# A deeper ring of split weights for SwiGLU, and silu in one ScalarE instruction, in a float32 encoder block on one core

## The chip, the cores and the metric

The kernel runs on one core of one Trainium2 chip. The metric is the device time of one execution in microseconds (us); lower is better. The median of three runs of the kernel before is 1158.89 us (1158.38 to 1160.23). About 0.2% of that, 2.3 us, is the bound used below between a change and no change.

The engines are named as in the profile: PE is TensorE's matmuls, PEld its weight loads, DVE is VectorE, ACT is ScalarE, POOL is GpSimd, and SP (SPq for its queue) is SyncE, which here issues the DMAs that bring the weights.

## The reference, cut to what matters

One encoder layer over 256 rows of width 2048: two kinds of attention heads side by side, a cross attention into 256 memory rows, and a SwiGLU feed-forward of hidden width 5632. All data is float32.

```python
x = x + concat(out_mla, out_diff) @ w_out
x = x + cross_attention(rms_norm(x), rms_norm(mem)) @ w_xo
hf = rms_norm(x, g_ffn)
x = x + (silu(hf @ w_gate) * (hf @ w_up)) @ w_down     # w_gate, w_up: 2048 x 5632
return rms_norm(x, g_final)
```

silu(v) is v times sigmoid(v). The change lies in the feed-forward and in the tile pools that it uses.

## The kernel before, in words

**Three matmuls for one.** A float32 operand is split into a high part of type float32r and the rest, so that each product is three matmuls (`mm`, L91 to L93: high by high, high by low, low by high). The split is two instructions (`split_into`, L99 and L100): ACT rounds the operand into the high tile, then DVE subtracts the high tile from the operand into the low tile. Every weight of the kernel passes through this split.

**The two rings.** A weight piece of 1 MB lands by one DMA from SP in a raw tile, `wraw` (128 x 2048 float32, a ring of 3). It is then split by 1024 columns into a tile `wh` and a tile `wl` (rings of 4 each). A ring's tile is taken again only after its last reader is done: a split waits until PE has used the tile four splits back, and a DMA waits until both parts of the raw tile three back have been split. The rings are in pool `wp` for the whole kernel; pool `act` (24 tiles) holds activations, and pool `sb` a ring of 7 small tiles called `nat` (128 x 512), used by attention and SwiGLU alike.

**Order of the work.** The program is handed to a planner that simulates the engines and fixes the order of instructions on each engine before the run; program order is the priority. DMAs of weights are kept in program order. In the trace, matmuls of neighbouring tiles are interleaved by that plan.

**SwiGLU.** It starts with 512 hidden columns done plainly (`narrow_chunk`: two projections of `x2T`, the unnormalized rows), during which the normalized and split rows `x2n` and `forms` are made (`normalized_pairs`). Then come five chunks of 1024 hidden columns (`wide_chunk`): a gate projection, silu of it, an up projection, the product `h`, and its transposes on PE. The chunks are in three groups (one narrow and one wide chunk, two wide, two wide), and each group ends with its part of the down projection. The last group's down projection ends the kernel, with the final norm.

**Plain and summed pairs.** A wide projection (`wide_project`) runs over pairs of 128-row blocks of the contraction. A plain pair takes 8 products (24 matmuls). A summed pair uses sums of weight blocks and of activation blocks, and takes 7 products (21 matmuls); it accumulates four of them apart, in PSUM tiles `q`, which five DVE instructions per projection join (L737 to L740 with an ACT copy L736, or their like in `wide_add`). Of the 8 pairs of a gate or up projection 2 are summed; the whole SwiGLU has 28 summed pairs. For a summed pair DVE makes sums of the raw weight blocks in a tile `tsum` (L707, L711, L712), and four splits follow: three into the ring, the last into an extra pair of tiles of its own (`wh2`, `wl2` in pool `wsum`, one each). `wsum` is opened where attention's pool `soft` has been closed.

**PSUM.** Eight banks: four `acc` tiles for accumulation and four `ps` tiles for `q`, for transposes and the like. The four `acc` tiles of the first wide projection are the ones that the narrow chunk's gate (`ga`) and up (`ua`) results leave.

**Silu.** In `narrow_chunk` ACT computes the sigmoid of the scaled accumulator into a `nat` tile `sg` (L808) and DVE multiplies accumulator, scale and `sg` (L809); a second DVE instruction multiplies by the up result into `h` (L811). In `wide_chunk`, four times per chunk, ACT computes the sigmoid into `sg` (L824) and DVE multiplies it onto the gate result (L825).

Of the kernel before, what the change touches and what calls it, by code (L numbers as in the profile page):

```python
# [19 lines left out]
P = 128  # L20
# [54 lines left out]
def encoder_block(ctx: ExitStack, tc: tile.TileContext, a, out):  # L75
    nc = tc.nc
    PS = bass.MemoryType.PSUM
    const = ctx.enter_context(tc.tile_pool(name="const", bufs=1))
    wp = ctx.enter_context(tc.tile_pool(name="wp", bufs=3))
# [4 lines left out]
    pps = ctx.enter_context(tc.tile_pool(name="pps", bufs=4, space=PS))  # L84
    tables = ExitStack()
    tp = tables.enter_context(tc.tile_pool(name="tp", bufs=1))


    def mm(o, l, r, start, stop):

        nc.tensor.matmul(o, l.h, r.h, start=start, stop=False)  # L91
        nc.tensor.matmul(o, l.h, r.l, start=False, stop=False)  # L92
        nc.tensor.matmul(o, l.l, r.h, start=False, stop=stop)  # L93
# [13 lines left out]
    def act_tile(shape=(P, 4, S), name="act"):  # L107
# [2 lines left out]
            act.tile(list(shape), F32R, name=name + "_l", tag="act"),  # L110
        )

    def weights(src, fine=False, pool=None, before_k=None, cut=None, raw=None):

        nk, ncols = src.shape[1:]
        begun = raw is not None
        if not begun:  # L120
            raw = wp.tile([P, 2048], F32, name="wraw", tag="wraw", bufs=3)
        raw = raw[:, :nk * ncols].rearrange("p (k c) -> p k c", k=nk)
        step = 1 if fine else nk
        for k in range(0, nk, step):
            if before_k is not None:
                before_k(k)
            if begun and k == 0:
                continue
            tc.keep_in_program_order(nc.sync.dma_start(out=raw[:, k:k + step, :], in_=src[:, k:k + step, :]))
        ks = []  # L130
        step = max(1, 1024 // ncols // 2 * 2)
        for k in range(0, nk, step):
            n = min(step, nk - k)
            if pool:
                w = pool((P, n, ncols), "w")
            else:
                w = [wp.tile([P, 1024], F32R, name=x, tag=x, bufs=4)[:, :n * ncols].rearrange("p (k c) -> p k c", k=n)
                     for x in ("wh", "wl")]
                w = Split(*w)
# [24 lines left out]
        return accs  # L164

    def nat(name):
        return sb.tile([P, 512], F32, name=name, tag="nat", bufs=7)

    def ps_tile(name):
        return pps.tile([P, 512], F32, name=name, tag="ps")  # L170
# [13 lines left out]


    LAT = KVL + DR
    lat_raw = wp.tile([P, 2048], F32, name="wraw", tag="wraw", bufs=3)
# [14 lines left out]
    posi = const.tile([P, NT], I32, name="posi")  # L202
    invf = const.tile([P, NF], F32, name="invf")
# [59 lines left out]

    posf = const.tile([P, NT], F32, name="posf")
    nc.gpsimd.tensor_copy(out=posf, in_=posi)
    ang = tp.tile([P, NT, NF], F32, name="ang")
    for tt in range(NT):
# [78 lines left out]
    cosr = const.tile([P, NT, 2, DR // 2], F32, name="cosr")  # L348
    sinr = const.tile([P, NT, 2, DR // 2], F32, name="sinr")
    cosd = const.tile([P, NT, 2, DD // 2], F32, name="cosd")  # L350
    sind = const.tile([P, NT, 2, DD // 2], F32, name="sind")

    def latents_normalized():
        cqs = [nat("cq") for _ in range(NT)]
# [152 lines left out]
    gdb = const.tile([P, DV], F32, name="gdb")  # L507
# [129 lines left out]
    def pair_raw(src):  # L637
        raw = wp.tile([P, 2048], F32, name="wraw", tag="wraw", bufs=3)
        raw = raw.rearrange("p (b c) -> p b c", b=4)
        tc.keep_in_program_order(nc.sync.dma_start(out=raw, in_=src))  # L640
        return raw

    def w_tile(n=2, pool=None):

        pool, tags, bufs = (wp, ("wh", "wl"), 4) if pool is None else (pool, ("wh2", "wl2"), 1)
        return Split(*[pool.tile([P, 1024], F32R, name=x, tag=x, bufs=bufs)[:, :n * 512].rearrange(
            "p (b c) -> p b c", b=n) for x in tags])

    def split_blocks(src, pool=None):
        w = w_tile(src.shape[1], pool)  # L650
        split_into(w, src)
        return w

    class Pair:

# [24 lines left out]
    def wide_project(pairs, src, order, leave, join):  # L680

        accs = [[pacc.tile([P, 512], F32, name="acc", tag="acc") for _ in range(2)] for _ in range(NT)]
        used = [[False] * 2 for _ in range(NT)]
        summed = [i for i in order if pairs[i].forms is not None]  # L690
        Q = {}
        for n, i in enumerate(order):
            stop = n == len(order) - 1
            raw = pair_raw(src[i])
            if i not in summed:
                w = [split_blocks(raw[:, 2 * k:2 * k + 2, :]) for k in range(2)]
                for tt in range(NT):
                    for oc in range(2):
                        for k in range(2):
                            mm(accs[tt][oc], pairs[i].at(k, tt), w[k][:, oc, :], not used[tt][oc], stop and k == 1)  # L700
# [6 lines left out]
            nc.vector.tensor_tensor(out=t[:, 0:2, :], in0=raw[:, 1:3, :],  # L707
                                    in1=raw[:, 0:1, :].to_broadcast([P, 2, 512]), op=ALU.add)
            t13 = split_blocks(t[:, 0:2, :])
            b21 = split_blocks(raw[:, 3:4, :])  # L710
            nc.vector.tensor_tensor(out=t[:, 2, :], in0=t[:, 0, :], in1=raw[:, 2, :], op=ALU.add)  # L711
            nc.vector.tensor_tensor(out=t[:, 3, :], in0=t[:, 2, :], in1=raw[:, 3, :], op=ALU.add)  # L712
# [3 lines left out]
            mm(Q[1], A11, b11[:, 0, :], *own)  # L716
            mm(accs[0][1], S3, b11[:, 1, :], False, stop)
            mm(Q[5], S5, t13[:, 0, :], *own)
            mm(Q[7], S7, t13[:, 1, :], *own)
            mm(accs[0][0], A12, b21[:, 0, :], False, stop)  # L720
            mm(Q[6], S6, t24[:, 0, :], *own)
            mm(accs[1][0], A22, t24[:, 1, :], False, stop)
# [76 lines left out]
    def narrow_chunk(c):  # L799

        ga = project(x2T, [a["w_gate0"][0, i] for i in range(4)])
        xn = normalized_pairs()
        ua = project(x2T, [a["w_up0"][0, i] for i in range(4)])
        t = act_tile(name="hT")
        for tt in range(NT):
            r = rstdf[:, tt:tt + 1]
            sg = nat("sg")
            nc.scalar.activation(sg, ga[tt], AF.Sigmoid, scale=r)  # L808
            nc.vector.scalar_tensor_tensor(out=sg, in0=ga[tt], scalar=r, in1=sg, op0=ALU.mult, op1=ALU.mult)  # L809
            h = nat("h")  # L810
            nc.vector.scalar_tensor_tensor(out=h, in0=ua[tt], scalar=r, in1=sg, op0=ALU.mult, op1=ALU.mult)  # L811
            transposed(t, h, tt, 4)
        return [Pair(t[:, 0:2, :]), Pair(t[:, 2:4, :])], xn
# [3 lines left out]
    def wide_chunk(c, spare):  # L817

        g = wide_result(xn, a["w_gu"][c, 0], GU_SEQ)
        for tt in range(NT):  # L820
            for oc in range(2):
                sg = nat("sg")
                gs = g[tt][:, oc, :]
                nc.scalar.activation(sg, gs, AF.Sigmoid)  # L824
                nc.vector.tensor_tensor(out=gs, in0=gs, in1=sg, op=ALU.mult)  # L825
        u = wide_result(xn, a["w_gu"][c, 1], GU_SEQ)
        t = act_tile(name="hT")
        pts = []
# [177 lines left out]
```

## Time and profile before

| quantity | value |
|---|---|
| median of the three runs | 1158.89 us |
| the profiled execution's own time | 1158.9 us |
| its span, first to last instruction | 1157.1 us |
| granted TensorE clock, mean | 0.999 |
| matmuls | 5510 |
| bytes moved by DMA | 222.13 MB, mean 192 GB/s |

The profile is a page about one execution, and a trace that can be asked for details. Durations of PE instructions overlap, since matmuls are pipelined and their ends are modelled; so the distance from one matmul's start to the next one's says more than its duration. In a row of a group of instructions, the columns are the source line, the engine, the operation, output and inputs by name, the shape, the count, then busy time in us, the mean of one in ns, and the idle time ahead of them with what ended it. In a row of a table by stage, each engine's busy time in us is followed by the number of its instructions in that stretch.

### The profile page before, as it was taken

The numbers are of one execution on the slowest core, as the hardware profiler recorded it, in microseconds if no ns is written. First come the engines' busy times: TensorE is split into PE (matmuls) and PEld (weight loads), VectorE is DVE, ScalarE is ACT, GpSimd is POOL, SyncE is SP. The second block draws the span as 40 slices with busy tenths as digits, with TensorE's granted clock in tenths as the row PEclk, the third lists the DMA queues.
The fourth block names the chain that finished last, engine by engine and source line by source line (L and its number), as shares of the span: only waits on it lengthen the run. The fifth ranks groups of instructions, "written<-read, shape, count | busy, mean of one in ns | idle before, by whom it ended". The sixth has DMA issues, their size and how long they took to land.

```text
span 1157.1 us, 14401 instructions
## 1 busy us (share of the span) xinstructions
PE 1148.1 (99%) x5510; PEld 961.7 (83%) x5510; DVE 901.3 (78%) x1197; ACT 611.0 (53%) x863; POOL 69.3 (6%) x81
## 2 busy tenths in 40 slices
PE   9999999999999999999999999999999999999997
PEld 7888888888888888888888888888888888888887
DVE  7698766586867776978888787797888788798873
ACT  6755454554665565655444554564544554554552
POOL 4920000001000000000000000000000000000021
PEclk9999999999999999999999999999999999999999
DMA  9565344435755445465565555645556555555651
GB/s 356 215 218 189 113 145 168 161 146 206 272 212 182 146 149 187 174 218 182 185 214 184 206 184 192 218 181 183 202 179 223 204 181 202 192 220 202 210 204 73
DMA packets 33764, 222.13 MB, mean 192 GB/s; under 512 B 4128, under 2 KB 4896, under 8 KB 8992
## 3 DMA queue, kind: packets, MB, share of 16 engines
q1 hardware_dynamic: 32256, 216.86, 52.4%
q0 software_dynamic: 864, 3.15, 0.7%
q10 hardware_dynamic: 576, 1.21, 0.3%
q8 instruction: 43, 0.70, 0.2%
q14 instruction: 25, 0.20, 0.1%
HBM read 219.11 MB, written 2.10 MB: 191 GB/s over the span
## 4 chain that ended last, share of the span: by engine, by line
PE 98%; DMA 1%; issue 0%; DVE 0%; SPq 0%; ACT 0%; POOLq 0%; POOL 0%; DVEq 0%; ACTq 0%
PE acc L92 28%; PE acc L91 28%; PE acc L93 28%; PE q L91 2%; PE q L92 2%; PE q L93 2%; PE pt L315 2%; PE ppt L462 1%; DMA wraw<-in_w_in_lat 1%; PE psc L93 1%; PE psc L91 1%; PE psc L92 1%; PE pt L838 0%; PE acckv L93 0%; PE acckv L92 0%
## 5 line engine op out<-in xcount | busy, mean ns | idle before, releaser
L99 ACT CAST wh<-wraw 128x1024 fp32r<-128x1024 f32 (+2 forms) x399 | 399.2, 1013 | 383.1 <-PE acc L93 346.7
L100 DVE TENSOR_TENSOR wl<-wraw,wh 128x1024 fp32r<-128x1024 f32 (+2 forms) x399 | 469.0, 1184 | 166.3 <-ACT wh L99 164.4
L92 PE MATMUL acc<-wl,x2n_h 128*128 128x512 f32 x480 | 185.5, 390 | 0.0
L93 PE MATMUL acc<-wh,x2n_l 128*128 128x512 f32 x480 | 185.2, 389 | 0.0
L91 PE MATMUL acc<-wh,x2n_h 128*128 128x512 f32 x480 | 160.3, 390 | 0.0
L93 PEld LDWEIGHTS acc<-wh,x2n_l 128*128 128x128 f32 x480 | 90.1, 188 | 18.8
L91 PEld LDWEIGHTS acc<-wh,x2n_h 128*128 128x128 f32 x480 | 90.1, 188 | 18.8
L92 PEld LDWEIGHTS acc<-wl,x2n_h 128*128 128x128 f32 x480 | 90.1, 188 | 18.7
L92 PE MATMUL acc<-wl,hT_h 128*128 128x512 f32 (+1 forms) x272 | 103.7, 381 | 0.0
L93 PE MATMUL acc<-wh,hT_l 128*128 128x512 f32 (+1 forms) x272 | 103.5, 381 | 0.0
L91 PE MATMUL acc<-wh,hT_h 128*128 128x512 f32 (+1 forms) x272 | 89.4, 382 | 0.0
L92 PE MATMUL acc<-wl,x0T_h 128*128 128x512 f32 x224 | 88.2, 395 | 0.0
L93 PE MATMUL acc<-wh,x0T_l 128*128 128x512 f32 x224 | 87.8, 393 | 0.0
L91 PE MATMUL acc<-wh,x0T_h 128*128 128x512 f32 x224 | 87.4, 396 | 0.3 <-ACT x0T_h L102 0.3
L99 ACT CAST wh<-tsum 128x1024 fp32r<-128x1024 f32 x56 | 58.3, 1047 | 42.2 <-DVE tsum L712 30.8
L100 DVE TENSOR_TENSOR wl<-tsum,wh 128x1024 fp32r<-128x1024 f32 x56 | 67.9, 1218 | 9.2 <-ACT wh L99 9.1
L91 PEld LDWEIGHTS acc<-wh,hT_h 128*128 128x128 f32 x272 | 51.2, 188 | 9.9 <-issue 0.2
L93 PEld LDWEIGHTS acc<-wh,hT_l 128*128 128x128 f32 x272 | 51.2, 188 | 9.6
L92 PEld LDWEIGHTS acc<-wl,hT_h 128*128 128x128 f32 x272 | 51.2, 188 | 9.4
L91 PEld LDWEIGHTS acc<-wh,x0T_h 128*128 128x128 f32 x224 | 42.2, 189 | 9.2 <-ACT x0T_h L102 1.2
L92 PEld LDWEIGHTS acc<-wl,x0T_h 128*128 128x128 f32 x224 | 42.3, 189 | 7.9 <-DVE wl L100 0.4
L93 PEld LDWEIGHTS acc<-wh,x0T_l 128*128 128x128 f32 x224 | 42.2, 188 | 7.6
(363 smaller groups left out, 2005.9 us busy)
## 6 DMA issues: line engine op xcount, KB each, us to landing
wraw<-in_w_gu SPq DMA_DIRECT2D x80, 1024.0 KB, 4.8
wraw<-in_w_dn SPq DMA_DIRECT2D x36, 1024.0 KB, 4.8
wraw<-in_w_in SPq DMA_DIRECT2D x24, 1024.0 KB, 4.8
wraw<-in_w_out SPq DMA_DIRECT2D x16, 1024.0 KB, 4.8
wraw<-in_w_down SPq DMA_DIRECT2D x8, 1024.0 KB, 4.8
wraw<-in_w_in_lat SPq DMA_DIRECT2D x7, 832.0 KB, 7.8
wraw<-in_w_xk SPq DMA_DIRECT2D x4, 1024.0 KB, 6.1
wraw<-in_w_xq SPq DMA_DIRECT2D x4, 1024.0 KB, 4.8
```

The costliest lines, as they stand in the source:

```text
L91: nc.tensor.matmul(o, l.h, r.h, start=start, stop=False)
L92: nc.tensor.matmul(o, l.h, r.l, start=False, stop=False)
L93: nc.tensor.matmul(o, l.l, r.h, start=False, stop=stop)
L99: last_cast[0] = nc.scalar.copy(out=dst.h, in_=src).ins
L100: last_split[0] = nc.vector.tensor_tensor(out=dst.l, in0=src, in1=dst.h.bitcast(F32), op=ALU.subtract).ins
L315: nc.tensor.transpose(out=pt[:, j * P:(j + 1) * P], in_=src[:, j * P:(j + 1) * P], identity=ident)
L462: nc.tensor.transpose(out=pt[:, kt * S + tt * P:kt * S + (tt + 1) * P], in_=p[:, tt, kt * P:(kt + 1) * P], identity=ident)
```

## The change

It does the following:

- `wraw`, `wh` and `wl` become `Ring` objects: lists of named slots of one tile each, taken in turn. A ring can be given more slots from another pool; the new ones are taken first.
- Tiles that only attention needs (`nat`, the rotary tables, `posi`, `invf`, `posf`, `gdb`) move to a pool `early`, which is closed with `soft` at the end of attention. In that space a pool `late` is opened: three more tiles `wh` and `wl` each, a ring of 3 `nat` tiles in place of 7, and `tsum` (three blocks in place of four).
- From SwiGLU on the rings of `wh` and `wl` have 7 tiles; the extra pair `wh2`, `wl2` goes. The ring of `wraw` keeps 3.
- The sums of a summed pair are made in another order, partly in place in the raw tile: two additions come before the pair's first split, two after it. The splits are of 1024, 1024, 1024 and 512 columns, all into the ring. The seven products keep their operands and come in another order.
- Silu is one ACT instruction with the function Silu. In `wide_chunk` it works in place on the gate result; the DVE product with the sigmoid goes.

```diff
-            raw = wp.tile([P, 2048], F32, name="wraw", tag="wraw", bufs=3)
+            raw = w_raw.next()
...
+    class Ring:
...
+        def more(self, pool, n):
+            self.slots = [(pool, f"{self.name}{self.made + i}") for i in range(n)] + self.slots
+            self.made += n
+        def next(self, name=None):
+            self.slots.append(self.slots.pop(0))
+            pool, tag = self.slots[-1]
+            return pool.tile([P, self.cols], self.dtype, name=name or self.name, tag=tag, bufs=1)
...
+    w_raw.more(wp, 3)
+    w_high.more(wp, 4)
+    w_low.more(wp, 4)
+    nat_pool = [early, 7]
...
     soft_pool.close()
-    wsum = ctx.enter_context(tc.tile_pool(name="wsum", bufs=1))
+    attention.close()
+    late = ctx.enter_context(tc.tile_pool(name="late", bufs=1))
+    nat_pool[:] = late, 3
+    w_high.more(late, 3)
+    w_low.more(late, 3)
...
-            t = wsum.tile([P, 4, 512], F32, name="tsum", tag="tsum", bufs=1)
-            b11 = split_blocks(raw[:, 1:3, :])
-            nc.vector.tensor_tensor(out=t[:, 0:2, :], in0=raw[:, 1:3, :],
-                                    in1=raw[:, 0:1, :].to_broadcast([P, 2, 512]), op=ALU.add)
-            t13 = split_blocks(t[:, 0:2, :])
-            b21 = split_blocks(raw[:, 3:4, :])
-            nc.vector.tensor_tensor(out=t[:, 2, :], in0=t[:, 0, :], in1=raw[:, 2, :], op=ALU.add)
-            nc.vector.tensor_tensor(out=t[:, 3, :], in0=t[:, 2, :], in1=raw[:, 3, :], op=ALU.add)
-            t24 = split_blocks(t[:, 2:4, :], wsum)
+            t = late.tile([P, 3, 512], F32, name="tsum", tag="tsum", bufs=1)
+            for o, x, y in ((t[:, 0, :], raw[:, 0, :], raw[:, 2, :]), (raw[:, 0, :], raw[:, 0, :], raw[:, 1, :])):
+                nc.vector.tensor_tensor(out=o, in0=x, in1=y, op=ALU.add)
+            t1, b11, b22, b21 = split_blocks(raw)
+            for o, x, y in ((t[:, 1, :], raw[:, 0, :], raw[:, 2, :]), (t[:, 2, :], t[:, 1, :], raw[:, 3, :])):
+                nc.vector.tensor_tensor(out=o, in0=x, in1=y, op=ALU.add)
+            t3, t2, t4 = split_blocks(t)
...
             sg = nat("sg")
-            nc.scalar.activation(sg, ga[tt], AF.Sigmoid, scale=r)
-            nc.vector.scalar_tensor_tensor(out=sg, in0=ga[tt], scalar=r, in1=sg, op0=ALU.mult, op1=ALU.mult)
+            nc.scalar.activation(sg, ga[tt], AF.Silu, scale=r)
...
-                sg = nat("sg")
-                gs = g[tt][:, oc, :]
-                nc.scalar.activation(sg, gs, AF.Sigmoid)
-                nc.vector.tensor_tensor(out=gs, in0=gs, in1=sg, op=ALU.mult)
+                nc.scalar.activation(g[tt][:, oc, :], g[tt][:, oc, :], AF.Silu)
```

More of the change, by code (lines that the diff above doesn't have):

```diff
@@ L84, in encoder_block @@
     pps = ctx.enter_context(tc.tile_pool(name="pps", bufs=4, space=PS))
+    attention = ExitStack()
+    early = attention.enter_context(tc.tile_pool(name="early", bufs=1))
     tables = ExitStack()
@@ L111, in act_tile, with __init__, split_tile @@
         )
+    class Ring:
+        def __init__(self, name, cols, dtype):
+            self.name, self.cols, self.dtype, self.slots, self.made = name, cols, dtype, [], 0
+        def more(self, pool, n):
[5 more added lines that the diff above has]
+            return pool.tile([P, self.cols], self.dtype, name=name or self.name, tag=tag, bufs=1)
+    w_raw, w_high, w_low = Ring("wraw", 2048, F32), Ring("wh", 1024, F32R), Ring("wl", 1024, F32R)
+    w_raw.more(wp, 3)
+    w_high.more(wp, 4)
+    w_low.more(wp, 4)
+    nat_pool = [early, 7]
+    def split_tile(n, ncols):
+        return Split(*[ring.next()[:, :n * ncols].rearrange("p (k c) -> p k c", k=n) for ring in (w_high, w_low)])
     def weights(src, fine=False, pool=None, before_k=None, cut=None, raw=None):
@@ L133, in weights @@
             n = min(step, nk - k)
[L134 to L139, printed above, removed]
+            w = pool((P, n, ncols), "w") if pool else split_tile(n, ncols)
             if fine:
@@ L166, in nat @@
     def nat(name):
-        return sb.tile([P, 512], F32, name=name, tag="nat", bufs=7)
+        pool, bufs = nat_pool
+        return pool.tile([P, 512], F32, name=name, tag="nat", bufs=bufs)
     def ps_tile(name):
@@ L186, in encoder_block @@
     LAT = KVL + DR
-    lat_raw = wp.tile([P, 2048], F32, name="wraw", tag="wraw", bufs=3)
+    lat_raw = w_raw.next()
     for c0, c1 in ((0, QL), (QL, QL + LAT)):
@@ L201, in encoder_block @@
     NF = DR // 2 + DD // 2
-    posi = const.tile([P, NT], I32, name="posi")
-    invf = const.tile([P, NF], F32, name="invf")
+    posi = early.tile([P, NT], I32, name="posi")
+    invf = early.tile([P, NF], F32, name="invf")
     ident = const.tile([P, P], F32, name="ident")
@@ L261, in encoder_block @@
                 mm(acc_kv[tt][:, :LAT], x, w[:, QL:], i + k == 0, i == 7 and k == 1)
-    posf = const.tile([P, NT], F32, name="posf")
+    posf = early.tile([P, NT], F32, name="posf")
     nc.gpsimd.tensor_copy(out=posf, in_=posi)
@@ L346, in encoder_block @@
     two_pi = float(np.nextafter(np.float32(2 * math.pi), np.float32(0)))
[L348 to L351, printed above, removed]
+    cosr = early.tile([P, NT, 2, DR // 2], F32, name="cosr")
+    sinr = early.tile([P, NT, 2, DR // 2], F32, name="sinr")
+    cosd = early.tile([P, NT, 2, DD // 2], F32, name="cosd")
+    sind = early.tile([P, NT, 2, DD // 2], F32, name="sind")
     def latents_normalized():
@@ L506, in encoder_block @@
                                    op0=ALU.add, op1=ALU.subtract)
-    gdb = const.tile([P, DV], F32, name="gdb")
+    gdb = early.tile([P, DV], F32, name="gdb")
     tc.keep_in_program_order(nc.sync.dma_start(out=gdb, in_=a["g_diff_sub"].partition_broadcast(P)))
@@ L633, in encoder_block, with split_blocks @@
     soft_pool.close()
-    wsum = ctx.enter_context(tc.tile_pool(name="wsum", bufs=1))
[L637 to L652, printed above, removed]
+    attention.close()
[3 more added lines that the diff above has]
+    w_low.more(late, 3)
+    def split_blocks(x):
+        blocks = []
+        for i in range(0, x.shape[1], 2):
+            n = min(2, x.shape[1] - i)
+            w = split_tile(n, 512)
+            split_into(w, x[:, i:i + n, :])
+            blocks += [w[:, j, :] for j in range(n)]
+        return blocks
     class Pair:
@@ L693, in wide_project @@
             stop = n == len(order) - 1
-            raw = pair_raw(src[i])
+            raw = w_raw.next().rearrange("p (b c) -> p b c", b=4)
+            tc.keep_in_program_order(nc.sync.dma_start(out=raw, in_=src[i]))
             if i not in summed:
-                w = [split_blocks(raw[:, 2 * k:2 * k + 2, :]) for k in range(2)]
+                w = split_blocks(raw)
                 for tt in range(NT):
@@ L699, in wide_project @@
                         for k in range(2):
-                            mm(accs[tt][oc], pairs[i].at(k, tt), w[k][:, oc, :], not used[tt][oc], stop and k == 1)
+                            mm(accs[tt][oc], pairs[i].at(k, tt), w[2 * k + oc], not used[tt][oc], stop and k == 1)
                             used[tt][oc] = True
@@ L704, in wide_project @@
                 Q = {q: ps_tile(f"q{q}") for q in (1, 5, 7, 6)}
[L705 to L713 removed]
+            t = late.tile([P, 3, 512], F32, name="tsum", tag="tsum", bufs=1)
[5 more added lines that the diff above has]
+            t3, t2, t4 = split_blocks(t)
             own = i == summed[0], i == summed[-1]
             A11, A12, A21, A22, S5, S6, S7, S3 = [pairs[i].forms[:, n, :] for n in range(8)]
[L716 to L722, printed above, removed]
+            mm(Q[1], A11, b11, *own)
+            mm(Q[5], S5, t1, *own)
+            mm(accs[0][1], S3, b22, False, stop)
+            mm(accs[0][0], A12, b21, False, stop)
+            mm(Q[7], S7, t3, *own)
+            mm(Q[6], S6, t2, *own)
+            mm(accs[1][0], A22, t4, False, stop)
             if i == summed[-1]:
```

2 lines of the change are left out of this document (1 added, 1 removed).

## The prediction

> **What bounds the kernel now.** I read the page first: the share of each engine, the span in slices, and the chain that ended last.
>
> ```profile
> span 1157.1 us, 14401 instructions
> ...
> PE 1148.1 (99%) x5510; PEld 961.7 (83%) x5510; DVE 901.3 (78%) x1197; ACT 611.0 (53%) x863; POOL 69.3 (6%) x81
> ...
> PE   9999999999999999999999999999999999999997
> ...
> PE 98%; DMA 1%; issue 0%; DVE 0%; SPq 0%; ACT 0%; POOLq 0%; POOL 0%; DVEq 0%; ACTq 0%
> ```
>
> TensorE is busy in every slice, and 98% of the chain lies on it. A busy share of matmuls can still hide waits, since one matmul's record overlaps the next one's. So I went on to the table by stage, for SwiGLU's steady part and for one stretch of 100 us without a transpose.
>
> ```profile
> 500.00:600.00 100.00, 100.00 (x449) 82.50 (x448) 82.24 (x101) 50.55 (x61) 0.00 (x0) 1.00 0.56 199
> 600.00:700.00 100.00, 100.00 (x441) 82.44 (x440) 80.99 (x91) 49.33 (x55) 0.00 (x0) 1.00 0.56 199
> ```
>
> The second row has 441 matmuls, all of 512 columns, in 100 us: one each 0.2268 us on average. The pace where one follows the other is read from the timeline of PE at the end of the narrow chunk:
>
> ```profile
> 475.61 0.39 PE L93 MATMUL acc<-wh,x2T_l 128*128 128x512 f32 x1
> ...
> 480.14 0.39 PE L93 MATMUL acc<-wh,x2T_l 128*128 128x512 f32 x1
> ```
>
> Twenty steps lie between these two starts (every row between shows one matmul, but for one that merges two): 4.53 / 20 = 0.2265 us. So 441 matmuls need 99.89 us at that pace, and the stretch of 100 us leaves 0.11 us in which TensorE could have waited. Then the waits, of PEld from 437 to 1146 us, of ACT and DVE from 500 to 1100 us, and of SP's queue over the same stretch:
>
> ```profile
> PEld acc L91 <- issue: 0.2, 1, 0.2
> ```
>
> ```profile
> ACT wh L99 <- PE acc L93: 232.3, 130, 7.1
> DVE wl L100 <- ACT wh L99: 82.4, 73, 3.5
> ```
>
> ```profile
> SPq L640 <- DVE wl L100: 535.3, 108, 8.9
> ```
>
> In 709 us of SwiGLU the matrix engine has one wait, of 0.2 us. The long waits all run the other way: ACT's splits wait for PE to free a tile, DVE for ACT, the DMAs for the splits. These are feeders that wait for the consumer, and none of that is on the path. So the ring of 4 and the extra pair already feed TensorE without a gap that the profile shows.
>
> **The change part by part.** *Matmuls.* A plain pair has 24 and a summed pair 21, before and after; only the order of the summed pair's seven products is new. 0 us.
>
> *What there is to win from waits.* The stretch from 475 to 1146 us is 671 us. At 0.11 us per 100 us it holds about 0.7 us of excess, and the ring can win no more than that there. I take 0.2 us, the one wait shown; the bounds are 0 and 0.7.
>
> *DVE's and ACT's work.*
>
> ```profile
> L100 DVE TENSOR_TENSOR wl<-tsum,wh 128x1024 fp32r<-128x1024 f32 x56 | 67.9, 1218 | 9.2 <-ACT wh L99 9.1
> L707 DVE TENSOR_TENSOR tsum<-wraw 128x1024 f32<-128x1024 f32 x28 | 34.1, 1218 | 2.9 <-DMA wraw<-in_w_dn 2.2 <-DMA wraw<-in_w_gu 0.2
> L712 DVE TENSOR_TENSOR tsum<-tsum,wraw 128x512 f32<-128x512 f32 x28 | 19.1, 683 | 0.2
> L711 DVE TENSOR_TENSOR tsum<-tsum,wraw 128x512 f32<-128x512 f32 x28 | 19.1, 683 | 0.1
> L825 DVE TENSOR_TENSOR res<-res,sg 128x512 f32<-128x512 f32 x20 | 13.1, 681 | 0.0
> L824 ACT ACTIVATE sg<-res 128x512 f32<-128x512 f32 x20 | 12.2, 627 | 9.1 <-DVE res L744 9.0
> L738 DVE TENSOR_TENSOR res<-q,res 128x512 f32<-128x512 f32 x10 | 6.9, 687 | 0.5
> ```
>
> The sums of a summed pair were 1.218 + 0.683 + 0.683 = 2.58 us and become four of 0.683, 2.73 us: 28 times 0.15 is 4.2 us more for DVE. The splits keep their sizes. Silu takes away 20 products of 0.681, 13.6 us, and two of 0.74 in the narrow chunk (L809, row below), 1.5 us. Net, DVE does 11 us less of its 901. ACT keeps 22 instructions; the trace has no Silu, so I bound it by ACT's cast of as many columns, 0.61 us, and the slowest sigmoid, 0.69 us (both in the fence on tables below), and take the sigmoid's 627 ns, whose shape it keeps; 22 times 0.06 would be 1.4 us more on ACT. None of this is on the path: a projection of 8 pairs costs PE 6 x 24 + 2 x 21 = 186 matmuls, 42.1 us, and costs DVE 12 splits of 1.218 (14.6), two summed pairs of 2.73 + 3 x 1.218 + 0.68 (14.1) and nine joins of 0.69 (6.2), 34.9 us. DVE stays the faster one. If the cover were gone, the 4.2 us would be the price. 0 us.
>
> *The first split of a summed pair now waits for two additions,* 1.37 us, where before its cast could go as soon as the raw tile had landed. ACT stands in order behind that cast. The plain pair ahead keeps PE for 24 x 0.2265 = 5.4 us, and with seven tiles the pairs ahead are split sooner; ACT is busy 50.55 of 100 us. 0 us, and 1.4 us each time if nothing were in hand.
>
> *Smaller ring of `nat`, and tiles that reuse attention's space.* `late` can be written when the last tiles of `early` and `soft` are done. The last softmax tile `e` is read by transposes, whose last one starts at 400.8 us, and the first gate product starts at 434.9 us, 34 us later:
>
> ```profile
> L462 PE MATMUL ppt<-ident,e x64: 270/272/273, 111.4 to 400.8; 128*128 128x128 f32 x64
> ```
>
> ```profile
> L91 PE MATMUL acc<-wh,x2T_h x64: 389/389/481, 434.9 to 479.7; 128*128 128x512 f32 x64
> ```
>
> So that hand-over costs 0 us. The `nat` ring of 3 is used in the order rb, rrow, two sums, sg, h, sg, h, so the second `sg` takes the tile of the second sums.
>
> ```profile
> 479.14 1.21 DVE L100 TENSOR_TENSOR wl<-wraw,wh 128x1024 fp32r<-128x1024 f32 x1
> 480.28 0.68 DVE L100 TENSOR_TENSOR forms_l<-sums,forms_h 128x512 fp32r<-128x512 f32 x1
> 480.88 0.74 DVE L811 SCALAR_TENSOR_TENSOR h<-acc,x2Tr,sg 128x512 f32<-128x512 f32 x1
> 481.54 0.68 DVE L100 TENSOR_TENSOR forms_l<-sums,forms_h 128x512 fp32r<-128x512 f32 x1
> 482.14 0.74 DVE L809 SCALAR_TENSOR_TENSOR sg<-acc,x2Tr,sg 128x512 f32<-128x512 f32 x1
> ```
>
> The second sums are last read at 481.54 + 0.68 = 482.22 us. A Silu of 0.68 us (the length of the sigmoid there, next fence) after that frees the gate's PSUM bank at 482.9 us; before, L809 frees it at 482.14 + 0.74 = 482.88 us. So the new wait ends where the removed product ended: 0 us, with the rival below for the case that it does not.
>
> *Activation tables.* ACT loaded a table ahead of the first sigmoid:
>
> ```profile
> 465.39 0.61 ACT L99 CAST x2n_h<-x2T_f 128x512 fp32r<-128x512 f32 x1
> 466.02 1.28 ACT L808 ACT_TABLE_LOAD   x1
> 467.31 0.69 ACT L808 ACTIVATE sg<-acc,x2Tr 128x512 f32<-128x512 f32 x1
> 467.90 0.70 ACT L99 CAST forms_h<-x2T_f 128x256 fp32r<-128x256 f32 x2
> ...
> 479.85 0.68 ACT L808 ACTIVATE sg<-acc,x2Tr 128x512 f32<-128x512 f32 x1
> ```
>
> Between the two sigmoids stand casts, and no second load. I expect one load of 1.28 us with Silu as well, 0 us on the path. The Trainium skill speaks against the change here: "ScalarE: Activation LUTs", in its section on table sets, says that a function outside the active set costs a switch of about 2.7 us, and that cheap functions such as copy are in every set. By its first half Silu between casts could switch back and forth; by its second it would not, and the casts above agree with the second.
>
> *Attention, head and tail* are not touched but for names of pools. The kernel's end, with the last product at 1149.56 us and 7.5 us of norm and store behind it, stays: 0 us.
>
> ```profile
> 1149.56 0.28 PE L93 MATMUL acc<-w_h,forms_l 128*128 128x256 f32 x1
> ```
>
> *Sum.* The profiled execution took 1158.9 us, 1157.1 of span and 1.8 around it, which is the median's 1158.89 too. 1158.9 - 0.2 = **1158.7 us**.
>
> **The rivals.** *One, the change does not do what it says (chance 0.12).* The ring of raw tiles stays at three, so with seven split tiles the splits may soon wait for DMAs in place of PE, and the feeders run hardly further ahead. For it speaks the row of SP's queue, whose DMAs wait for splits; against it, that 1 MB lands in 4.8 us:
>
> ```profile
> wraw<-in_w_gu SPq DMA_DIRECT2D x80, 1024.0 KB, 4.8
> ```
>
> A pair takes PE 4.8 to 5.4 us, so the landing keeps pace. The time would be 1158.9 us, also no change.
>
> *Two, slower (0.10).* At SwiGLU's start DVE is the tight engine:
>
> ```profile
> 475.00:500.00 25.00, 25.00 (x116) 20.64 (x115) 23.08 (x28) 13.68 (x17) 0.00 (x0) 1.00 0.50 175
> ```
>
> It is busy 23.08 of 25 us. The three new tiles let the planner put up to three more weight splits of 1.21 us ahead of the `forms_l` subtractions. Then the small `nat` ring holds the second Silu, and so the PSUM bank of the gate, 3 x 1.21 = 3.6 us longer. Two products per pair (6 matmuls, 1.36 us) can run on one free bank, so it decides from a delay of about 1.4 us on. In full it gives 1158.9 + 3.6 = 1162.5 us. Against it: the extra splits would more likely fill ACT's and DVE's idle time before 475 us, and take load off this stretch.
>
> *Three, faster by another order (0.06).* The planner fixes a new order of PE's work. The stretch from 500 to 600 us holds 16 transposes:
>
> ```profile
> L315 PE MATMUL pt<-ident,res x8: 270/272/273, 568.5 to 572.0; 128*128 128x128 f32 x8
> L838 PE MATMUL pt<-ident,res x8: 272/273/273, 572.1 to 573.3; 128*128 128x128 f32 x8
> ```
>
> Its other 433 matmuls take 98.07 us at 0.2265, which leaves 1.93 / 16 = 0.12 us per transpose, where 128 columns at the pace of 512 would be 0.057. If the new order put the 88 of SwiGLU (16 per wide chunk, 8 of the narrow one) singly between long matmuls, it would win up to 88 x 0.064 = 5.6 us: 1153.3 us. Nothing in the change moves transposes, though.
>
> *Four, faster because TensorE is not full (0.02).* If the pace of 0.2265 us were set by feeding and not by the array, weight loads, busy 82.5 of 100 us, would leave up to 17.5%; over 671 us that is 117 us, 1041 us. The same pace with DVE at 81 to 92% busy speaks against it. By the Trainium skill ("Perfetto Trace Analysis", Identifying the Most-Contended Engine) weight-load busy is the measure of headroom and matmul busy is not; this trace's even starts with no waits say that this headroom is not one that buffers can reach.
>
> **How the numbers follow.** The forecast has 0.70 and rival one 0.12, both within 0.2% (2.3 us, about what a measurement of this kernel can tell from no change): same 0.82. Rival two gives slower 0.10, three and four faster 0.08. The runs of before spread from 1158.4 to 1160.2; the range takes in that spread, the 0.7 us to win, and about a third of rivals two's and three's prices: 1156.6 to 1161.4 us.
>
> **What would show it right or wrong.** Right: 441 matmuls per 100 us in stretches without transposes, DVE's busy time near 890 us, ACT's wait for PE moved but still long, one table load at the first Silu, no row of PEld waiting over 0.5 us. Wrong: PEld waiting for `wh` or `wl`, above all between 465 and 500 us; a second table load; fewer matmuls per 100 us; a PE order with transposes apart from each other.

## The result, and the profile after

The change makes the kernel slower by 0.8%: a median of 1168.55 us in six runs (1167.67 to 1169.09), beside 1159.41 us for the kernel before in six runs (1158.38 to 1160.23). The ratio is 1.0079 with a 95% interval of 1.0067 to 1.0090. The forecast of 1158.7 us, no change, was wrong, and the result lies above its range. The two profiled spans differ by 8.7 us, 1165.8 against 1157.1.

The page of after, its share of engines and its chain:

```profile
span 1165.8 us, 14417 instructions
...
PE 1156.2 (99%) x5510; PEld 961.4 (82%) x5510; DVE 890.9 (76%) x1203; ACT 609.1 (52%) x863; POOL 67.9 (6%) x81
...
PE 98%; issue 0%; DMA 0%; DVE 0%; ACT 0%; POOLq 0%; POOL 0%; DVEq 0%; ACTq 0%
```

The same 5510 matmuls keep TensorE busy for 99% of a span that is longer, and the chain still lies on it. The table by stage of after says how:

```profile
475.00:500.00 25.00, 25.00 (x114) 20.35 (x114) 19.59 (x26) 12.50 (x15) 0.00 (x0) 1.00 0.42 149
500.00:600.00 100.00, 100.00 (x444) 81.81 (x443) 79.52 (x97) 50.64 (x60) 0.00 (x0) 1.00 0.55 196
600.00:700.00 100.00, 100.00 (x435) 81.42 (x434) 79.54 (x93) 48.05 (x53) 0.00 (x0) 1.00 0.54 198
```

From 600 to 700 us the row counts 435 matmuls where before it counted 441, at a granted clock of 1.00 in both. DVE is less busy than before in all three stretches. Is TensorE waiting? From 437 to 1155 us the waits of PEld have no row at all. The waits of ACT, DVE and SP's queue in after, from 500 to 1100 us, say the same:

```profile
ACT wh L101 <- PE acc L95: 202.8, 78, 5.4
```

```profile
DVE wl L102 <- ACT wh L101: 97.1, 62, 5.1
```

```profile
SPq L717 <- DVE wl L102: 520.6, 105, 11.7
```

The feeders wait for TensorE, as before. So no wait has come; the matmuls themselves have become slower, and not all of them. Two stretches from the timeline of PE in after show it. In the first every matmul reads a weight tile of the new pool `late`:

```profile
692.72 0.40 PE L93 MATMUL acc<-wh,x2n_h 128*128 128x512 f32 x1
692.95 0.39 PE L94 MATMUL acc<-wl,x2n_h 128*128 128x512 f32 x1
...
699.50 0.40 PE L95 MATMUL q<-wh,forms_l 128*128 128x512 f32 x1
```

In the second every matmul reads one of the four old ring tiles:

```profile
929.05 0.39 PE L94 MATMUL acc<-wl,x2n_h 128*128 128x512 f32 x1
...
937.44 0.39 PE L95 MATMUL acc<-wh,x2n_l 128*128 128x512 f32 x1
```

The first has 29 steps in 6.78 us, 0.2338 us each; the second has 37 in 8.39 us, 0.2268 us each. The operation, the shapes and the kinds of operand are the same. The modelled duration of 0.39 to 0.40 us doesn't tell them apart; only the distance between starts does.

The trace of before had this already, in a place that the prediction did not read: the four matmuls that read the extra pair, and what follows them.

```profile
547.12 0.39 PE L92 MATMUL q<-wl,forms_h 128*128 128x512 f32 x1
547.35 0.40 PE L93 MATMUL q<-wh,forms_l 128*128 128x512 f32 x1
547.59 0.40 PE L92 MATMUL acc<-wl,forms_h 128*128 128x512 f32 x1
547.83 0.39 PE L93 MATMUL acc<-wh,forms_l 128*128 128x512 f32 x1
548.06 0.39 PE L92 MATMUL q<-wl,forms_h 128*128 128x512 f32 x1
548.28 0.39 PE L93 MATMUL q<-wh,forms_l 128*128 128x512 f32 x1
```

From 547.12 to 548.06 us lie four steps of 0.235 us on average; the next is 0.22 us.

So the question for the experiments was: what is it about a tile's place that costs a matmul 6 ns? A tile's place is its start in bytes within a partition, which the built program gives. Before, the rings of `wh` and `wl` lie at 62976 to 95744, the activations (`act`, the stationary operands) from 95744, and the extra pair at 219296 and 223392. After, the old ring tiles lie at 42048 to 83008, `act` from 91200, and the six new tiles from 192224 up, 4096 apart.

### The profile page after: what moved, and what is told of

Read it like the earlier page. It is cut to its first block, busy times and chain, and to the rows that moved or that the text cites. A ratio compares the mean times of both kernels' runs of the same rounds, so it can differ in the third digit from the quotient of the medians.

```text
span 1165.8 us, 14417 instructions
## 1 busy us (share of the span) xinstructions
PE 1156.2 (99%) x5510; PEld 961.4 (82%) x5510; DVE 890.9 (76%) x1203; ACT 609.1 (52%) x863; POOL 67.9 (6%) x81
## 4 chain that ended last, share of the span: by engine, by line
PE 98%; issue 0%; DMA 0%; DVE 0%; ACT 0%; POOLq 0%; POOL 0%; DVEq 0%; ACTq 0%
PE acc L94 28%; PE acc L93 28%; PE acc L95 28%; PE q L94 2%; PE q L95 2%; PE q L93 2%; PE pt L340 2%; PE ppt L487 1%; PE psc L95 1%; PE psc L94 1%; PE psc L93 1%; PE acckv L93 0%; PE acckv L95 0%; PE acckv L94 0%; PE pt L856 0%
## 5 line engine op out<-in xcount | busy, mean ns | idle before, releaser
L102 DVE TENSOR_TENSOR wl<-wraw,wh 128x1024 fp32r<-128x1024 f32 (+2 forms) x399 | 478.6, 1216 | 151.9 <-ACT wh L101 149.8
L101 ACT CAST wh<-wraw 128x1024 fp32r<-128x1024 f32 (+2 forms) x399 | 407.3, 1042 | 348.9 <-PE acc L95 281.9
L93 PE MATMUL acc<-wh,x2n_h 128*128 128x512 f32 x480 | 183.9, 394 | 0.0
L93 PE MATMUL acc<-wh,hT_h 128*128 128x512 f32 (+1 forms) x272 | 102.2, 384 | 0.0
L102 DVE TENSOR_TENSOR wl<-tsum,wh 128x1024 fp32r<-128x1024 f32 (+1 forms) x56 | 52.9, 953 | 36.6 <-ACT wh L101 35.7
L101 ACT CAST wh<-tsum 128x1024 fp32r<-128x1024 f32 (+1 forms) x56 | 46.5, 832 | 53.2 <-PE acc L95 41.3
```

The costliest lines, as they stand in the source:

```text
L101: last_cast[0] = nc.scalar.copy(out=dst.h, in_=src).ins
L102: last_split[0] = nc.vector.tensor_tensor(out=dst.l, in0=src, in1=dst.h.bitcast(F32), op=ALU.subtract).ins
```

## The experiments

There are four theories. (1) The deeper ring itself: seven tiles in flight, or the new order of PE's work, slow the matmuls down. (2) Silu or its freed DVE time does. (3) The place of the moving operand: its start, being an odd multiple of 32 bytes (192224, 219296), or its lying high in memory. (4) Something between the places of the two operands; this one grew out of the first runs. But for `b3` and `d1`, each kernel has the order of instructions, on every engine, of the kernel that it is made from; only addresses differ, but for the pad's memset on POOL. Each was timed beside the kernel before on the same chip (1159.01, 1159.03 and 1159.12 us in the three batches, in the order of the text).

**`a1_late_aligned`**: the changed kernel, with 32 bytes ahead of the tiles of `late`, which then start at 192256.

```diff
+    nc.gpsimd.memset(late.tile([P, 8], F32, name="pad", tag="pad", bufs=1), 0.0)
```

> The changed kernel with one unused tile of 32 bytes put first in the pool late, so that its tiles start at multiples of 64 bytes (192256 in place of 192224); every engine has the same instructions in the same order as in the changed kernel, but for one memset on POOL. Theory of the start address (a matmul whose moving operand starts at an odd multiple of 32 bytes takes some 6.5 ns longer, 233.5 in place of 227): the 8.7 us of slower matmuls in SwiGLU go, and the time is 1168.55 - 8.7 = 1159.9 us or up to 1 us less. Theory of the high address (tiles above 190000 bytes are slower to read, wherever they start): no change, 1168.5 us. Theory of the deeper ring (splits that run further ahead disturb PE's reads): no change, 1168.5 us.

**`b1_extra_aligned`**: the kernel before, with the same 32 bytes ahead of the extra pair, in `wsum`.

> The kernel before with the same 32 bytes put first in the pool wsum, so that the extra pair wh2, wl2 starts at a multiple of 64 bytes. Theory of the start address: 168 matmuls read that pair; 168 x 6.5 ns = 1.1 us, and up to 0.5 us for the matmuls right behind them, so 1.1 to 1.6 us less than before. Theories of the high address and of the deeper ring: no change.

**`b2_rings_off32`**: the kernel before, with 32 bytes ahead of the split rings in `wp` (and 32 in `act`, so that `act` stays a multiple of 64 away from zero): rings from 63008, `act` from 95808.

```diff
+    for pool in (wp, act):
+        nc.gpsimd.memset(pool.tile([P, 8], F32, name="pad", tag="pad", bufs=1), 0.0)
```

> The kernel before with 32 unused bytes between the raw tiles and the rings wh and wl, and 32 more behind them, so that the rings' tiles, at low addresses from 63008 on, start at odd multiples of 32 bytes and the pool act at multiples of 64 as before. Same order of instructions. Theory of the start address: nearly all 4476 matmuls of 512 columns and some 250 shorter ones read a ring tile as moving operand; at 6.5 ns each about 29 to 31 us more, 1188 us (1184 to 1192). Theory of the high address: no change, 1159 us. Theory of the deeper ring: no change, 1159 us.

**`b3_silu_only`**: the kernel before with the Silu of the change and nothing else.

```diff
-                nc.scalar.activation(sg, gs, AF.Sigmoid)
-                nc.vector.tensor_tensor(out=gs, in0=gs, in1=sg, op=ALU.mult)
+                nc.scalar.activation(g[tt][:, oc, :], g[tt][:, oc, :], AF.Silu)
```

> The kernel before with Silu in one ScalarE instruction, and nothing else of the change: ring of 4, extra pair, nat ring of 7. Theories of the start address, of the high address and of the deeper ring: within 1 us of before, since Silu touches no ring. A theory that Silu (a table switch, or the order that the planner makes with it) costs the time: 1168 us.

The stretch from 600 to 700 us in the table by stage, one fence for each, in the order above:

```profile
600.00:700.00 100.00, 100.00 (x435) 81.19 (x434) 79.53 (x93) 47.99 (x53) 0.00 (x0) 1.00 0.54 198
```

```profile
600.00:700.00 100.00, 100.00 (x441) 82.55 (x440) 81.15 (x91) 49.50 (x55) 0.00 (x0) 1.00 0.55 199
```

```profile
600.00:700.00 100.00, 100.00 (x431) 80.53 (x430) 82.71 (x94) 47.15 (x51) 0.00 (x0) 1.00 0.55 192
```

```profile
600.00:700.00 100.00, 100.00 (x440) 82.27 (x440) 79.61 (x88) 49.62 (x55) 0.00 (x0) 1.00 0.58 200
```

`a1` took 1167.19 us (ratio 1.0070, 1.0058 to 1.0083) and `b1` 1158.75 us (0.9995, 0.9987 to 1.0004): starting at a multiple of 64 bytes heals neither. `b2` took 1182.59 us (1.0203, 1.0184 to 1.0221), with the old ring, the old order and 431 matmuls where before has 441. So a place alone can cost 2%. It cost less than the 1188 us (1184 to 1192) that was expected: a matmul loses 5.8 ns and not 6.5, as the count below has it, and shorter matmuls lose nothing. The new tiles of `a1` start at multiples of 64 bytes and are slow, the rings of before start at such multiples and are fast: the start of the moving tile by itself is not the rule. `b3` took 1159.12 us (1.0001, 0.9991 to 1.0010): Silu takes DVE from 81.0 to 79.6 us in the stretch and brings and costs nothing.

**`d1_raws_high`**: the changed kernel with the three raw tiles in `late` from SwiGLU on, and the three new pairs where the raw tiles were, at 33856 to 91200 beside the old ones. The ring is still of 7, with Silu.

```diff
-    w_high.more(late, 3)
-    w_low.more(late, 3)
+    old_raws = w_raw.slots
+    w_raw = Ring("wraw_late", 2048, F32)
+    w_raw.more(late, 3)
...
+            pair = pool.tile([P, 2048], F32R, name="whl", tag=tag, bufs=1)
+            both = pair[:, :1024], pair[:, 1024:]
```

> The changed kernel with two roles exchanged: from SwiGLU on the three raw tiles lie in the pool late (192224 bytes and up), and the three extra pairs of wh and wl lie where the raw tiles were (33856 to 91200, multiples of 64). The ring has seven pairs, Silu and the nat ring of 3 stay. Theory of the place (a moving operand in a tile at a high address, or starting at an odd multiple of 32 bytes, costs a matmul some 6.5 ns): no tile of the rings is slow any more, so the 8.7 us go and the time is 1158 to 1160 us. Theory of the deeper ring: no change, 1167 to 1169 us.

**`d2_rings_at_128k`** and **`d3_rings_above_act`**: the kernel before with its pools in another order, so that the rings lie at 114816 to 147584, and at 161280 to 194048, in both above the activations.

The edit of `d2` follows; `d3` leaves `const` first and puts `rp`, `act` and `wp` behind it, in this order.

```diff
+    act = ctx.enter_context(tc.tile_pool(name="act", bufs=24))
+    wp = ctx.enter_context(tc.tile_pool(name="wp", bufs=4))
     const = ctx.enter_context(tc.tile_pool(name="const", bufs=1))
-    wp = ctx.enter_context(tc.tile_pool(name="wp", bufs=3))
-    act = ctx.enter_context(tc.tile_pool(name="act", bufs=24))
+    rp = ctx.enter_context(tc.tile_pool(name="rp", bufs=3))
...
-            raw = wp.tile([P, 2048], F32, name="wraw", tag="wraw", bufs=3)
+            raw = rp.tile([P, 2048], F32, name="wraw", tag="wraw", bufs=3)
```

> The kernel before with its pools in another order in memory: act lowest, then the rings, at 114816 to 147584 bytes (multiples of 64), then constants and raw tiles. Same order of instructions. The tiles wh lie below 131072, the tiles wl above; all of them above the activations, which are the stationary operands. Theory of a fixed line for the moving operand's address: if the line is at 131072 bytes, the matmuls with wl as moving operand (a third, about 1500) take 6.5 ns longer, 10 us, 1169 us; if it is higher than 147584, no change, 1159 us; if it is lower than 114816, all of them, 29 us, 1188 us. Theory of the relative place (moving above stationary is slow): all, 1188 us. Theory of the deeper ring: no change.

> The kernel before with the rings above act, at 161280 to 194048 bytes (multiples of 64), activations at 62976 to 161280. Same order of instructions. Theory of a fixed line: below 161280, all matmuls with a ring tile take 6.5 ns longer, 1183 to 1188 us; with a line inside the rings only the tiles above it do, and the intervals by tile show where it lies. Theory of the relative place: 1183 to 1188 us. Theory of the deeper ring: no change, 1159 us.

**`b4_act_off32`**: the kernel before with 32 bytes ahead of the activations. The rings stay at 62976, and `act` starts at 95776.

```diff
+    for pool in (act, sb):
+        nc.gpsimd.memset(pool.tile([P, 8], F32, name="pad", tag="pad", bufs=1), 0.0)
```

> The kernel before with 32 unused bytes at the start of act, and 32 behind it, so that the activations (stationary in SwiGLU and in all projections, moving only in attention's short matmuls) start at odd multiples of 32 bytes and the rings at multiples of 64 as before. Same order of instructions. Theory of the place of the moving operand: within 2 us of before. A theory that the place of either operand counts, or the difference of their starts: about as slow as with the rings moved by 32, 1182 us.

The same stretch of `d1`, then of `b4`:

```profile
600.00:700.00 100.00, 100.00 (x443) 82.81 (x442) 81.24 (x94) 50.26 (x56) 0.00 (x0) 1.00 0.55 199
```

```profile
600.00:700.00 100.00, 100.00 (x431) 80.54 (x430) 82.60 (x94) 47.65 (x52) 0.00 (x0) 1.00 0.54 191
```

`d1` took 1156.77 us (0.9979, 0.9970 to 0.9988). It has the ring of seven, Silu and the new sums, and no loss: theory 1 falls (as it does by `a2` below, which has the very order of the changed kernel). `d2` (ratio 1.0000, 0.9990 to 1.0010) and `d3` (1.0001, 0.9991 to 1.0011) each took 1159.06 us: how high a ring lies, and on which side of the activations, makes no difference. `b4` took 1181.97 us (1.0195, 1.0176 to 1.0214), though no weight tile of its rings had moved: theory 3 falls too. Moving the stationary tiles by 32 bytes costs what moving the moving tiles does. What is left is the distance between the starts of a matmul's two operands.

In before and `b3` the rings are a multiple of 256 bytes away from `act`. The extra pair, and the new tiles of after, are a multiple of 256 plus 160 away (219296 - 95744 = 482 x 256 + 160; 192224 - 91200 = 394 x 256 + 160). The tiles of `act`, and the pieces of 512 columns in a ring tile, are all multiples of 256 apart, so one remainder holds for all of a pool. This theory made four more kernels. Two bring remainders to 0 by 96 bytes, one tries 128, and one moves both operands alike.

**`a2_late_by_96`**: the changed kernel, with the tiles of `late` from 192320.

```diff
+    nc.gpsimd.memset(late.tile([P, 24], F32, name="pad", tag="pad", bufs=1), 0.0)
```

> The changed kernel with 96 unused bytes (in place of a1's 32) put first in late, so that its tiles start at 192320: the distance from the activations' tiles is then a multiple of 128 (and of 256, not of 512). Same order of instructions as in the changed kernel. Theory of the distance, with a period of 128 bytes (a matmul of 512 columns takes some 6 ns longer when the starts of its moving and its stationary operand do not agree modulo 128): all slow matmuls go, and the time is that of d1, 1157 us (1156 to 1158.5). With a period of 256: the same. With a period of 512: as the changed kernel, 1167 to 1169 us. Theory that the start alone counts (a multiple of 64): as a1, 1167 us. Theory that a ring in late is slow because of its high address: 1167 us.

**`c4_extra_by_96`**: the kernel before, with the same pad in `wsum`, so that the extra pair starts at 219392.

> The kernel before with 96 unused bytes put first in wsum, so that the extra pair lies a multiple of 128 from the activations. Same order of instructions. Theory of the distance: the 168 matmuls with the extra pair fall from 232.8 to 227.5 ns, 0.9 us, and some of those behind them, 0.5 us: 1.0 to 1.5 us less than before, near 1157.7 us. Theories of the start alone and of the high address: no change.

**`c1_act_off128`**: the kernel before, with 128 bytes ahead of the activations.

```diff
+    nc.gpsimd.memset(act.tile([P, 32], F32, name="pad", tag="pad", bufs=1), 0.0)
```

> The kernel before with 128 unused bytes at the start of act, so that activations and rings differ by an odd multiple of 128. Same order of instructions. Theory of the distance with a period of 128 bytes: no change, 1159 us. With a period of 256 or more: as with a shift of 32, 1182 us.

**`c3_both_off32`**: the kernel before, with 32 bytes ahead of the rings, which moves the activations by as much (rings from 63008, `act` from 95776).

```diff
+    for pool in (wp, sb):
+        nc.gpsimd.memset(pool.tile([P, 8], F32, name="pad", tag="pad", bufs=1), 0.0)
```

> The kernel before with 32 unused bytes ahead of the rings, so that rings and activations both start at odd multiples of 32 and agree modulo 128. Same order of instructions. Theory of the distance: no change, 1159 us. Theory of the start alone: 1182 us, as with either of them shifted.

The same stretch of `a2`, `c4`, `c1` and `c3`, in this order:

```profile
600.00:700.00 100.00, 100.00 (x442) 82.78 (x442) 81.22 (x95) 50.27 (x56) 0.00 (x0) 1.00 0.54 198
```

```profile
600.00:700.00 100.00, 99.98 (x441) 82.52 (x441) 81.20 (x91) 49.58 (x55) 0.00 (x0) 1.00 0.57 200
```

```profile
600.00:700.00 100.00, 100.00 (x433) 81.03 (x432) 83.08 (x95) 45.83 (x51) 0.00 (x0) 1.00 0.56 200
```

```profile
600.00:700.00 100.00, 100.00 (x441) 82.51 (x441) 81.14 (x91) 49.32 (x55) 0.00 (x0) 1.00 0.56 199
```

| kernel | us, median | ratio to before | 95% interval |
|---|---|---|---|
| `a2_late_by_96` | 1157.21 | 0.9981 | 0.9972 to 0.9990 |
| `c4_extra_by_96` | 1156.79 | 0.9980 | 0.9971 to 0.9989 |
| `c1_act_off128` | 1178.89 | 1.0168 | 1.0149 to 1.0186 |
| `c3_both_off32` | 1158.36 | 0.9993 | 0.9983 to 1.0003 |

All four went as the distance says. Ninety-six bytes take the changed kernel from 1168.55 to 1157.21 us. In `c3` both operands start at odd multiples of 32 and nothing is lost. In `c1` both start at multiples of 128 and 1.7% is lost, so agreeing modulo 128 is not enough. In `a2` and `c4` the distance is an odd multiple of 256 (192320 - 91200 = 395 x 256), so agreeing modulo 512 is not needed. A period of 256 bytes fits all of these runs. `c4` won somewhat more than the estimate of 1.0 to 1.5 us for its 168 matmuls; its span is 1.3 us shorter, and the interval of its ratio just holds 1.3 us.

One count over the traces of all fourteen kernels puts a size on it: the interval from one start to the next where a matmul of 512 columns stands between two others of 512, grouped by the distance between its own operands, modulo 256 bytes. Intervals of 250 ns and more, which hold a wait, are left out.

| remainder, bytes | intervals | mean, ns |
|---|---|---|
| 0 | 42,957 | 227.4 |
| 32 | 168 | 233.5 |
| 128 | 4,065 | 232.5 |
| 160 | 2,133 | 233.3 |
| 192 | 1,797 | 233.0 |
| 224 | 8,130 | 233.2 |

The mean at remainder 0 is a mixture. In `a2`, where every weight tile agrees, 3,930 of 4,231 intervals are 224 to 229 ns long; the other 301 are near 233 ns, and 251 of these lie within six matmuls behind a wait or a matmul of another width. What makes those slow is not shown.

The prices close. In `b2`, 4,065 intervals by 233.3 - 227.5 = 5.8 ns are 23.6 us, and it is 23.6 us above before (1182.59 - 1159.01). In `c1`, 4,065 by 5.0 are 20.3 us, and it is 19.8 above.

What no run tells: why the chip does this; whether the moving tile must agree with the stationary tile of its own matmul or with that of the next one, which is loaded meanwhile (in before the weight load of the matmul at 929.37 us runs from 929.15 to 929.33, beside the matmul that starts at 929.14; all stationary tiles of these matmuls lie in `act` and agree with each other, so the two distances are one); remainders of 64 and 96 at 512 columns, and shifts under 32 bytes. Of other widths, matmuls of 320 and of 256 columns showed no loss (the operands of the latter differ in more than the distance).

## Why the prediction was wrong

**The step that failed** is "*Matmuls.* A plain pair has 24 and a summed pair 21, before and after; only the order of the summed pair's seven products is new. 0 us." The count was right, 5510 in both. The pace of 0.2265 us was taken from one stretch, in which all weight tiles agree with the activations, and used as a constant of the instruction. It is a property of where the operands lie, and the change moved weight tiles to another place. Of the intervals counted above, before has 4,065 at remainder 0 (mean 227.5 ns) and 168 at 160 (232.8). After has 2,938 at 0 (228.0; those right behind a slow one lose a little too) and 1,293 at 160 (233.8). So 1,293 x 6.3 ns is 8.1 us, 2,938 x 0.5 is 1.5, less 168 x 5.3 = 0.9 that before already paid: 8.7 us, the difference of the spans. The prediction treated "tiles that reuse attention's space" as a question of when that space is free. That was right and cost nothing; it did not ask where the space lies.

**One sum hid the first sign.** The prediction took 441 matmuls by 0.2265 us as 99.89 us and saw 0.11 us of excess. But a row counts every matmul that overlaps its stretch. 439 start between 600 and 700 us, and from the first of these starts to the one behind the last are 99.98 us: the excess is 99.98 - 439 x 0.2265 = 0.55 us. Of this, 0.20 us lies on the 30 matmuls that read the extra pair. So the "0.7 us" that waits could hold at most was too small, and part of the excess was no wait at all.

**The markers worked one way only.** 435 matmuls per 100 us in place of 441 was named as a sign of the prediction being wrong. The signs given beside it (PEld waiting, a second table load, transposes apart) did not come. A pace that falls with no wait was not among the cases.

**Rival four** asked whether the pace is set by feeding and not by the array, and priced it only as a gain by buffers. The runs show no such gain. But a part of the pace does hang on where the operands lie: 6 of 233 ns. The Trainium skill ("SBUF — State Buffer", Who interferes with whom) gives PE one read port for the moving operand and an independent one for weight loads, and says that PE never waits on anyone. That names no cost for any pair of places, and by it alone `b4` would take 1159 us; it took 1182. The same page (Operand start alignment) ties a start only to the element's size and says that this is about legality, not speed; here the speed needs more than the legal start.

**Rival one** (raw tiles limit the run-ahead) did not take the gain away. With the addresses agreeing, `d1` and `a2` (1156.8 and 1157.2 us) are 0.2% faster than before, but `c4` gets 1156.8 with the old ring and the sigmoid. So that 0.2% can be had from the place of the extra pair alone. On top of it the deeper ring and Silu bring nothing that can be measured. A longer run-ahead had no wait of TensorE to remove.

**Rival two** did not come. At SwiGLU's start DVE is busy 19.59 of 25 us (23.08 before), and the hand-over of the `nat` tile runs nearly as worked out, in the timelines of DVE and then of ACT in after:

```profile
480.27 0.69 DVE L102 TENSOR_TENSOR forms_l<-sums,forms_h 128x512 fp32r<-128x512 f32 x1
...
481.47 0.69 DVE L102 TENSOR_TENSOR forms_l<-sums,forms_h 128x512 fp32r<-128x512 f32 x1
```

```profile
481.67 1.05 ACT L101 CAST wh<-tsum 128x1024 fp32r<-128x1024 f32 x1 [0.58 <-DVE tsum L734]
482.62 0.68 ACT L830 ACTIVATE sg<-acc,x2Tr 128x512 f32<-128x512 f32 x1
```

The prediction had the second subtraction at 481.54 us, lasting 0.68. The Silu behind it stood behind a weight cast too: it ends at 483.30 us and not at 482.9. These 0.4 us are less than the 1.4 us that the rival needed, and PEld shows no wait. **Rival three** did not come either: with the addresses agreeing, `a2` has the new order and is no faster than `c4` with the old one.

**The small steps were right.** DVE fell to 890.9 us (forecast: near 890). The four sums of a summed pair and Silu, from the groups of DVE and of ACT in after, from 475 to 1160 us:

```profile
L734 DVE TENSOR_TENSOR tsum<-tsum,wraw 128x512 f32<-128x512 f32 x28 | 19.3, 688 | 0.5
L731 DVE TENSOR_TENSOR tsum<-wraw 128x512 f32<-128x512 f32 x28 | 19.3, 688 | 1.3 <-DMA wraw<-in_w_gu 0.9
L734 DVE TENSOR_TENSOR tsum<-wraw 128x512 f32<-128x512 f32 x28 | 19.2, 687 | 0.5
L731 DVE TENSOR_TENSOR wraw<-wraw 128x512 f32<-128x512 f32 x28 | 19.2, 686 | 0.3
```

```profile
L843 ACT ACTIVATE res<-res 128x512 f32<-128x512 f32 x20 | 12.5, 629 | 10.0 <-DVE res L766 10.0
```

Four sums of 0.69 us (forecast 0.683) and a Silu of 629 ns (forecast 627). The timeline of ACT in after has one table load ahead of the first Silu and none later in SwiGLU:

```profile
466.93 1.28 ACT L830 ACT_TABLE_LOAD   x1
468.22 0.69 ACT L830 ACTIVATE sg<-acc,x2Tr 128x512 f32<-128x512 f32 x1
```

So the half of the rule that the prediction drew from the Trainium skill ("ScalarE: Activation LUTs", Table sets: the hidden batching unit), that cheap functions are in every set, agrees with this trace for Silu between casts. The Silu starts 0.01 us after the load's end, so the switch took 1.29 us here and not the 2.7 us that the prediction quotes.

## What to carry to other kernels

Where TensorE is the bound and shows no wait, look at the distance between matmul starts tile by tile before calling the pace a constant: a pace that differs by tile is a hint that the busy share, the waits and the modelled durations all hide. When a change moves matmul operands or makes new tiles for them, work out where they land. On this chip, 512-column float32r matmuls went best with both operands' starts equal modulo 256 bytes, and a small pad of 96 bytes was worth more than three more pairs of buffers. And a buffer ring is deepened for a wait that the profile shows; here there was none.

## What the runs showed of the hardware that had not been expected

Behind a 512-column float32r matmul the next one starts 227.4 ns later on average when the moving and the stationary operand of the first start at the same remainder modulo 256 bytes, and 232.5 to 233.5 ns later at each other distance that was seen (remainders 32, 128, 160, 192, 224). At these five remainders the price is nearly the same: it does not grow with the distance. The absolute start (`c3`), the height in memory (`d2`, `d3`) and which of the two operands is moved (`b2`, `b4`) make no difference that these runs can measure. Over this whole kernel the times lie between 1157 us, where all weight tiles agree, and 1183 us, where none does.
